# Strassen weight sums as additions, two of the four made by accumulating DMA transfers, in a decoder block on one core

## The chip, the cores and the metric

The kernel runs on one core of a Trainium2 chip. The metric is the device time of one execution in microseconds (us). TensorE (PE) does matrix products, VectorE (DVE) sums and differences of tiles, ScalarE (ACT) casts and activations, GpSimd (POOL) and SyncE (SP) mostly issue DMA transfers, each from a queue of its own that it works off in order.

## The reference

A hybrid decoder block on x of 512 positions by 2048 channels, in float32:

```python
proj = x @ w_in                       # 2048 x 7168
u_conv, u_pool, gates = proj[:, :2048], proj[:, 2048:3072], sigmoid(proj[:, 3072:])
y_conv = swish(layer_norm(causal_conv31(glu(u_conv)))) @ w_conv_out
y_pool = multiscale_pool(u_pool) @ w_pool * pool_scale
mix = (g_conv * y_conv + g_pool * y_pool) @ w_out
h = layer_norm(alpha * x + mix)
g, up = split(h @ w_ffn_in)           # 2048 x 11264
f = (silu(g) * up) @ w_ffn_out        # 5632 x 2048
out = layer_norm(alpha * h + f)
```

## The kernel before

Everything is laid out with channels on the 128 partitions. Each product is made in three passes over parts of type float32r: an operand is split into hi (a cast on ScalarE, line 85) and lo (the rest, a subtraction on VectorE, line 86), and a product is hi hi + hi lo + lo hi. Most stages run plain matmuls of 512 columns. Two stages, seven of the ten groups of gates (4 granules each) and the feed-forward's first product (22 groups of 4 granules), use Strassen's scheme in Winograd's form: the halves of positions, of input channels and of columns are 2 x 2 blocks, and seven products, numbered 1 to 7, of sums of input blocks by sums of weight blocks take the place of eight. A product of one granule is 12 matmuls of 256 columns, a granule 84. A group collects its seven products in seven PSUM banks over its four granules, and then drains them into sums (line 447 on VectorE). The products 1 and 2, which need unsummed weight blocks only, are done ahead in the first three feed-forward groups (EARLY = 3, `first_products`), so that these groups' granules have five products left, 60 matmuls. The input's sums are made once, by `sum_x` for the gates and `sum_s` for the feed-forward.

The weights come as a stream of blocks. `weights(n)` hands out block n; in a Strassen stage it prepares block n + 1 and loads block n + 2 before that. `load` (line 149) issues two transfers of 512 KB on SP's queue for a granule: (B11, B21) and (B12, B22). `combine` makes the four sums from them, all subtractions on VectorE (line 177), in a chain:

```python
sub(t1, b12, b11)
sub(t3, b22, b12)
sub(t2, b22, t1)
sub(t4, b21, t2)
```

Three of the four results take the place of a raw block; t2 goes to a small tile of its own (`unit`). Tiles come from the pool `pairs` (`d`, 46 buffers of 4 KB per partition), smaller ones from `units` (`u`, 10 of 2 KB). A framework places instructions on the engines and sets semaphores; what follows which on an engine is set when the program is built. GpSimd issues the stores of results that are read again later: gates, `conv`, `kept` (line 578) and `act` (line 664).

Of the kernel before, what the change touches and what calls it, by code (L numbers as in the profile page):

```python
# [18 lines left out]
P = 128  # L19
# [15 lines left out]
PLAIN = 3  # groups of gates whose product is plain  # L35
TAPS_AHEAD = 6

# columns of the packed per-channel parameters
# [12 lines left out]
def block_kernel(ctx, tc, xT, x, w1, wgs, wpool, wconv, wout, wfs, wfo, prm, rows, out):  # L51
    """Products run in three passes over float32r parts: a = hi + lo exactly, a b = hi hi + hi lo + lo hi.

    The feed-forward's first product goes through Strassen's scheme in Winograd's form, with the
    halves of positions, of input channels and of columns (gate, up) as its 2 x 2 blocks.
    """
    nc = tc.nc
    const = ctx.enter_context(tc.tile_pool(name="const", bufs=1))
    dp = ctx.enter_context(tc.tile_pool(name="pairs", bufs=46))
    up = ctx.enter_context(tc.tile_pool(name="units", bufs=10))  # L60
# [7 lines left out]
    def unit(dt=F32, shape=(512,)):  # L68
        return up.tile([P, *shape], dt, tag="u", name="u")

# [23 lines left out]
    def halves(ts):  # L94
        """Pairs as the list of their single tiles."""
        return [t[:, i, :] for t in ts for i in range(2)]

# [26 lines left out]
    for s in range(EARLY):  # L124
        use["fe", s] = len(blocks)
        blocks.extend(wfs[s, g, 0] for g in range(4))
# [16 lines left out]
    def load(n):  # L143
        if n < len(blocks) and n not in raw:
            src = blocks[n]
            if in_strassen(n):
                ts = [pair(shape=(2, 2, 256)) for _ in range(2)]
                for i in range(2):
                    nc.sync.dma_start(ts[i], src[i])
                raw[n] = ts  # L150
                return
            t = pair(shape=src.shape[1:])
            for k in (0, 1) if n == 0 else (slice(0, 2),):
                nc.sync.dma_start(t[:, k], src[:, k])
            raw[n] = t
# [14 lines left out]

    def combine(t, early):
        """The seven sums of weight blocks of Winograd's form, in parts, by the number of the product;
        without the first two where they are in use already."""
        b1, b2 = t
        b11, b21, b12, b22 = b1[:, 0], b1[:, 1], b2[:, 0], b2[:, 1]
        t1, t4, t3, t2 = b11, b21, b12, unit(shape=(2, 256))
        sub = lambda o, p, q: nc.vector.tensor_tensor(o, p, q, op=ALU.subtract)  # L177
        if not early:
            h1, l1 = split(b1)
        sub(t1, b12, b11)  # L180
        sub(t3, b22, b12)
        sub(t2, b22, t1)
        sub(t4, b21, t2)
        h2, l2 = unit(F32R, (2, 256)), unit(F32R, (2, 256))
        split_into(h2, l2, t2)
        h3, l3 = split(b2)
        h4, l4 = split(b1)
        ops = {6: (h2, l2), 7: (h3[:, 0], l3[:, 0]), 3: (h3[:, 1], l3[:, 1]),
               5: (h4[:, 0], l4[:, 0]), 4: (h4[:, 1], l4[:, 1])}
        if not early:  # L190
            ops.update({1: (h1[:, 0], l1[:, 0]), 2: (h1[:, 1], l1[:, 1])})
        return ops
# [21 lines left out]
    def spread(items, n):  # L214
        """The items in order over n steps."""
        return [items[i * len(items) // n:(i + 1) * len(items) // n] for i in range(n)]

    def channel_major(at, n_blocks, hi, lo, ps=None, half=None, during=()):
        """Weights stationary: four tiles of output channels by positions."""
        ps = ps or [bank() for _ in range(4)]  # L220
        sl = slice(0, 512) if half is None else slice(H * half, H * half + H)
        during = spread(during, n_blocks)
        for g in range(n_blocks):
            for f in during[g]:
                f()
            wh, wl = weights(at + g)
            for k in range(2):
                kt = 2 * g + k
                for c in range(4):
                    cs = slice(c * P, (c + 1) * P)  # L230
                    first = g == 0 and k == 0
                    last = g == n_blocks - 1 and k == 1
                    o = ps[c][:, sl]
                    nc.tensor.matmul(o, lhsT=wh[:, k, cs], rhs=hi[kt], start=first, stop=False)  # L234
                    nc.tensor.matmul(o, lhsT=wh[:, k, cs], rhs=lo[kt], start=False, stop=False)  # L235
                    nc.tensor.matmul(o, lhsT=wl[:, k, cs], rhs=hi[kt], start=False, stop=last)  # L236
        return ps

    def position_major(at, n_blocks, hi, lo, tbs, during=()):
        """Activations stationary: blocks of 128 positions by 512 output channels."""  # L240
# [17 lines left out]
    def mean_rstd(stats):  # L258
        """stats [P, n, 6] -> mean and 1/sqrt(var + eps).

        Three Newton steps y <- -y/2 (v y^2 - 3). The factor -1/2 of each is left out of y and put
        into v of the next (64 v, 16 v, 4 v) and into the start, which is -1/8 of the usual guess.
        """
# [44 lines left out]
    def conv_taps(u, c):  # L308
        """u, acc: one tile of channels by positions; the taps are queued."""
        u, acc = u  # L310

        def first():
            nc.scalar.activation(acc, u, AF.Identity, scale=col(C_DW + c * TAPS + TAPS - 1), bias=col(C_DWB + c))

        def tap(s):
            nc.vector.scalar_tensor_tensor(acc[:, s:], u[:, :S - s], col(C_DW + c * TAPS + TAPS - 1 - s),  # L316
                                           acc[:, s:], op0=ALU.mult, op1=ALU.add)

        background.append(first)
        for s in range(1, TAPS):  # L320
            background.append(lambda s=s: tap(s))
# [19 lines left out]
    # gates of the two branches, inputs of the pooling  # L341
# [10 lines left out]
    def pool_pair(i):  # L352
        """The steps for a pair of channel tiles."""
# [61 lines left out]
    def sum_x(i):  # L415
        """Winograd's sums of blocks of the input, for the channel tiles 2 i, 2 i + 1 of each half."""
# [3 lines left out]
        for o, a, b, op in ((a22, a21, a22, ALU.add), (a21, a11, a21, ALU.subtract),  # L420
                            (a11, a22, a11, ALU.subtract), (a12, a12, a11, ALU.subtract)):
            nc.vector.tensor_tensor(o, a, b, op=op)
# [9 lines left out]
    def products(ns, w, g, ps, operand):  # L432
        for n in ns:
            wh, wl = w[n]
            for j in range(2):
                h, l = operand(n, g, j)
                for p in range(2):
                    cs = slice(p * P, (p + 1) * P)
                    o = ps[n][:, p * H:(p + 1) * H]
                    # the start clears the marks of its whole bank, so one group spans both tiles  # L440
# [4 lines left out]

    def add(o, p, q):
        nc.vector.tensor_tensor(o, p, q, op=ALU.add)  # L447
# [17 lines left out]
    def strassen_gates(s, during=()):  # L465
# [10 lines left out]
        add(a, ps[6], a)  # L476
# [4 lines left out]
        add(b, ps[4], b)  # L481
# [59 lines left out]
    # by halves of the positions and tiles of 4 x 128 channels: whole, high part, low part  # L541
    af, ahi, alo = {}, {}, {}

    def norm1(t):
        """The steps of LayerNorm for a block of positions, into the layout by channels."""
# [6 lines left out]
        def chunk(c):  # L552
# [5 lines left out]
            parts = half == 0 or c > 1  # the fourth block goes into sums only  # L558
# [40 lines left out]
    def sum_s(i):  # L599
        """Winograd's sums of blocks of the input, for the channel tiles i and i + 2."""  # L600
        # each in the place of a block that is not needed whole any more
        a11, a12, a21, a22 = (0, i), (0, i + 2), (1, i), (1, i + 2)

        def step(n, o, a, b, op):
# [3 lines left out]
        return [lambda: step(1, a22, a21, a22, ALU.add), lambda: step(3, a21, a11, a21, ALU.subtract),  # L608
                lambda: step(2, a11, a22, a11, ALU.subtract), lambda: step(4, a12, a12, a11, ALU.subtract)]

    def operand(n, g, j):
        """The input's block or sum of the product n for a channel tile of the granule."""
# [8 lines left out]
    def gate1(ps, a, c11):  # L621
        """The sum of the first product, and the gate of the first half of the positions."""
# [6 lines left out]
    def first_products(s, during):  # L629
        ps = {n: bank() for n in (1, 2)}  # L630
        during = spread(during, 4)
        for g in range(4):
# [3 lines left out]
            products((1, 2), {1: (h[:, 0], l[:, 0]), 2: (h[:, 1], l[:, 1])}, g, ps, operand)  # L636
# [3 lines left out]
    def strassen_ffn(s, during=()):  # L640
# [13 lines left out]
        add(a, ps[6], a)  # L654
# [5 lines left out]
        add(b, ps[4], b)  # L660
# [36 lines left out]
    def restore(t, i):  # L697
        """Adds the scaled residual to the sums of a pair of column chunks."""
# [20 lines left out]
    def norm2(t):  # L719
        """The steps of the last LayerNorm for a block of positions."""  # L720
# [62 lines left out]
    # the last run goes block by block of positions  # L783
# [26 lines left out]
def _granules(w, cols):  # L810
    """[K, N] -> [len(cols), K/256, 128, 2, 512] with the given columns in each block."""
# [5 lines left out]
def _strassen_granules(w):  # L817
    """[K, 2, n, 256] -> [n, 4, 2 column halves, 128, 2 channel halves, 2, 256]."""
    w = w.reshape(2, 4, 2, P, *w.shape[1:])
    return w.transpose(5, 1, 4, 3, 0, 2, 6)  # L820
# [48 lines left out]
```

## Time and profile before

| | |
|---|---|
| median of 2 runs | 2304.68 us (2304.14 to 2305.23) |
| span of the profiled execution | 2303.7 us |
| TensorE busy | 2263.2 us, 98% |
| VectorE busy | 1657.7 us, 72% |
| ScalarE busy | 806.8 us, 35% |
| GpSimd busy | 132.0 us, 6% |
| read from HBM | 284.36 MB |

A row of busy time says how long an engine's instructions ran, not that anything waited for them. The chain that ended last says on what the end rests, and the waits of an engine say what it stood still for. Windows give the same numbers for one stretch of the execution, with the clock that TensorE was granted (PEclk: 1.00 is 2.4 GHz, 0.50 is 1.2 GHz) and the share of the 16 DMA engines in use.

### The profile page before, as it was taken

Reading aid. Unit: us, or ns where it says so; the run is one execution under the profiler, and the core shown is the slowest. Engines: PE = TensorE matmul, PEld = TensorE weight load, DVE = VectorE, ACT = ScalarE, POOL = GpSimd, SP = SyncE. Lnnn points to the kernel's source line nnn. Section 1 sums busy time; section 2 is a strip of 40 time slices with the busy share of each in tenths; the row PEclk is TensorE's granted clock in tenths of the full one; section 3 lists DMA queues with packets and bytes.
Section 4 is the critical chain, followed back from the end, with each engine's and each line's share of the span. In section 5 each row is a group of like instructions: output and inputs, shape, how many; then the busy total and the mean of one; then the engine's idle time right before and its main releaser. Section 6 shows DMA issues by size and latency. Waiting matters only on the chain.

```text
span 2303.7 us, 35226 instructions
## 1 busy us (share of the span) xinstructions
PE 2263.2 (98%) x14576; PEld 2072.1 (90%) x14576; DVE 1657.7 (72%) x2139; ACT 806.8 (35%) x952; POOL 132.0 (6%) x139
## 2 busy tenths in 40 slices
PE   8999999999999999799999999999999999999997
PEld 7888889999988888799999999999999888888885
DVE  4999788878677358989878787887878426363337
ACT  3212253444323236334434344343434333222211
POOL 0000000000000002400000000000000000000005
PEclk9999999999999999899999999999999999999998
DMA  6232253334746355243333333333334635454321
GB/s 259 90 102 76 101 204 128 134 119 158 272 157 218 110 181 203 92 158 121 117 128 112 109 129 119 112 118 128 112 109 142 211 105 201 134 172 135 108 83 73
DMA packets 90448, 319.15 MB, mean 139 GB/s; under 512 B 10544, under 2 KB 10672, under 8 KB 90288
## 3 DMA queue, kind: packets, MB, share of 16 engines
q1 hardware_dynamic: 77040, 273.71, 35.2%
q0 software_dynamic: 8352, 28.32, 3.2%
q10 hardware_dynamic: 4896, 14.88, 1.8%
q8 instruction: 114, 1.87, 0.3%
q14 instruction: 46, 0.38, 0.1%
HBM read 284.36 MB, written 32.51 MB: 138 GB/s over the span
## 4 chain that ended last, share of the span: by engine, by line
PE 93%; DVE 4%; issue 1%; ACT 1%; DMA 1%; POOL 0%; ACTq 0%; DVEq 0%
PE ps L444 16%; PE ps L442 16%; PE ps L443 16%; PE ps L775 6%; PE ps L776 6%; PE ps L774 6%; PE ps L236 5%; PE ps L235 5%; PE ps L234 5%; PE ps L253 3%; PE ps L254 3%; PE ps L255 3%; DVE d L86 1%; DVE d L177 1%; DMA d<-xT 1%
## 5 line engine op out<-in xcount | busy, mean ns | idle before, releaser
L86 DVE TENSOR_TENSOR d<-d 128x1024 fp32r<-128x1024 f32 (+1 forms) x607 | 736.7, 1231 | 397.1 <-ACT d L85 266.7
L85 ACT CAST d<-d 128x1024 fp32r<-128x1024 f32 (+1 forms) x615 | 630.1, 1047 | 885.5 <-DVE d L177 207.3
L444 PE MATMUL ps<-d 128*128 128x256 f32 x2784 | 788.4, 284 | 14.6 <-DVE d L86 14.3
L442 PE MATMUL ps<-d 128*128 128x256 f32 x2784 | 789.2, 284 | 1.4 <-ACT d L85 1.4
L443 PE MATMUL ps<-d 128*128 128x256 f32 x2784 | 788.7, 284 | 0.0
L444 PEld LDWEIGHTS ps<-d 128*128 128x128 f32 x2784 | 535.1, 193 | 16.7 <-DVE d L86 16.7
L442 PEld LDWEIGHTS ps<-d 128*128 128x128 f32 x2784 | 536.3, 193 | 1.9 <-ACT d L85 1.9
L443 PEld LDWEIGHTS ps<-d 128*128 128x128 f32 x2784 | 536.2, 193 | 0.1
L774 PE MATMUL ps<-d 128*128 128x512 f32 x640 | 249.0, 389 | 0.0
L775 PE MATMUL ps<-d 128*128 128x512 f32 x640 | 249.0, 389 | 0.0
L776 PE MATMUL ps<-d 128*128 128x512 f32 x640 | 248.1, 389 | 0.0
L234 PE MATMUL ps<-d 128*128 128x512 f32 x608 | 238.2, 392 | 5.1 <-ACT d L85 5.1
L235 PE MATMUL ps<-d 128*128 128x512 f32 x608 | 238.3, 392 | 1.6 <-DVE d L304 1.0
L236 PE MATMUL ps<-d 128*128 128x512 f32 x608 | 236.1, 392 | 0.4 <-DVE d L86 0.4
L447 DVE TENSOR_TENSOR u<-ps,u 128x512 f32<-128x512 f32 x188 | 127.1, 689 | 84.2 <-PE ps L444 81.8
L177 DVE TENSOR_TENSOR d<-d 128x512 f32<-128x512 f32 x232 | 167.6, 722 | 7.8 <-DMA d<-wfs 0.9
L316 DVE SCALAR_TENSOR_TENSOR d<-d,pr 128x510 f32<-128x510 f32 (+26 forms) x240 | 161.5, 765 | 0.6
L774 PEld LDWEIGHTS ps<-d 128*128 128x128 f32 x640 | 120.1, 188 | 25.0
L775 PEld LDWEIGHTS ps<-d 128*128 128x128 f32 x640 | 120.1, 188 | 24.9
L776 PEld LDWEIGHTS ps<-d 128*128 128x128 f32 x640 | 120.1, 188 | 24.9
L234 PEld LDWEIGHTS ps<-d 128*128 128x128 f32 x608 | 114.9, 189 | 28.4 <-ACT d L85 5.0
L235 PEld LDWEIGHTS ps<-d 128*128 128x128 f32 x608 | 114.8, 189 | 26.7 <-DVE d L86 1.5
(113 smaller groups left out, 2249.4 us busy)
## 6 DMA issues: line engine op xcount, KB each, us to landing
d<-wfs SPq DMA_DIRECT2D x188, 512.0 KB, 4.2
d<-wfo SPq DMA_DIRECT2D x88, 512.0 KB, 3.6
d<-wgs SPq DMA_DIRECT2D x56, 512.0 KB, 4.3
d<-w SPq DMA_DIRECT2D x55, 512.0 KB, 3.7
d<-wout SPq DMA_DIRECT2D x48, 512.0 KB, 3.9
d<-act SPq DMA_DIRECT2D x22, 512.0 KB, 4.6
act<-u POOLq DMA_DIRECT2D x41, 256.0 KB, 5.0
d<-gate SPq DMA_DIRECT2D x20, 512.0 KB, 4.7
```

The lines of the kernel that those rows point to most:

```text
L85: nc.scalar.copy(hi, src)
L86: (engine or nc.vector).tensor_tensor(lo, src, f32(hi), op=ALU.subtract)
L177: sub = lambda o, p, q: nc.vector.tensor_tensor(o, p, q, op=ALU.subtract)
L234: nc.tensor.matmul(o, lhsT=wh[:, k, cs], rhs=hi[kt], start=first, stop=False)
L235: nc.tensor.matmul(o, lhsT=wh[:, k, cs], rhs=lo[kt], start=False, stop=False)
L236: nc.tensor.matmul(o, lhsT=wl[:, k, cs], rhs=hi[kt], start=False, stop=last)
L442: nc.tensor.matmul(o, lhsT=wh[:, j, cs], rhs=h, start=first, stop=False)
L443: nc.tensor.matmul(o, lhsT=wh[:, j, cs], rhs=l, start=False, stop=False)
L444: nc.tensor.matmul(o, lhsT=wl[:, j, cs], rhs=h, start=False, stop=last)
L774: nc.tensor.matmul(ps[t], lhsT=hi[k][:, ts], rhs=wh[:, k, :], start=first, stop=False)
L775: nc.tensor.matmul(ps[t], lhsT=hi[k][:, ts], rhs=wl[:, k, :], start=False, stop=False)
L776: nc.tensor.matmul(ps[t], lhsT=lo[k][:, ts], rhs=wh[:, k, :], start=False, stop=last)
```

## The change

All four sums of weight blocks become additions. For that the sums of the input change their signs (`sum_x`, `sum_s`), and in the drain two additions become subtractions (products 6 and 4). The blocks of a granule lie in memory as B12, B22, B21, B11. A granule is loaded with three transfers: `t31` = (B22, B11) on SP's queue, 512 KB in pieces of 2 KB; then, on GpSimd's queue, an accumulating transfer that adds B12 to both halves of `t31`, so that it holds (B22 + B12, B11 + B12); and the triple `w3` = (B22, B21, B11) on SP's queue, 768 KB. VectorE makes the other two sums, `t24`, each from the one before it. Splits are then made of `t24`, of `t31` (1024 columns each) and of the triple (1536 columns, 512 in the early groups). The pools are recut: 40 pairs, 6 triples of 6 KB, 4 units.

```diff
-    dp = ctx.enter_context(tc.tile_pool(name="pairs", bufs=46))
-    up = ctx.enter_context(tc.tile_pool(name="units", bufs=10))
+    dp = ctx.enter_context(tc.tile_pool(name="pairs", bufs=40))
+    tp = ctx.enter_context(tc.tile_pool(name="triples", bufs=6))
+    up = ctx.enter_context(tc.tile_pool(name="units", bufs=4))
...
+    def triple(dt=F32):
+        return tp.tile([P, 3, 2, 256], dt, tag="w3", name="w3")
...
-        blocks.extend(wfs[s, g, 0] for g in range(4))
+        blocks.extend(wfs[s, g, :, 2:4] for g in range(4))
...
-                ts = [pair(shape=(2, 2, 256)) for _ in range(2)]
-                for i in range(2):
-                    nc.sync.dma_start(ts[i], src[i])
-                raw[n] = ts
+                w3, t31 = triple(), pair(shape=(2, 2, 256))
+                nc.sync.dma_start(t31, src[:, 1::2])
+                nc.gpsimd.dma_start(t31, src[:, 0:1].broadcast_to([P, 2, 2, 256]), accum_op=ALU.add)
+                nc.sync.dma_start(w3, src[:, 1:])
+                raw[n] = w3, t31
                 return
...
+        w3, t31 = t
+        w22, w21 = w3[:, 0], w3[:, 1]
+        t24 = pair(shape=(2, 2, 256))
+        add(t24[:, 0], t31[:, 1], w22)
+        add(t24[:, 1], t24[:, 0], w21)
+        h2, l2 = split(t24)
+        h1, l1 = split(t31)
+        h3, l3 = triple(F32R), triple(F32R)
+        n3 = 1 if early else 3
+        split_into(h3[:, :n3], l3[:, :n3], w3[:, :n3])
+        ops = {6: (h2[:, 0], l2[:, 0]), 4: (h2[:, 1], l2[:, 1]), 7: (h1[:, 0], l1[:, 0]), 5: (h1[:, 1], l1[:, 1])}
+        ops.update({n: (h3[:, i], l3[:, i]) for i, n in enumerate((3, 2, 1)[:n3])})
         return ops
...
-        for o, a, b, op in ((a22, a21, a22, ALU.add), (a21, a11, a21, ALU.subtract),
-                            (a11, a22, a11, ALU.subtract), (a12, a12, a11, ALU.subtract)):
+        for o, a, b, op in ((a22, a21, a22, ALU.subtract), (a21, a21, a11, ALU.subtract),
+                            (a11, a11, a22, ALU.subtract), (a12, a12, a11, ALU.subtract)):
...
-        add(a, ps[6], a)
+        sub(a, ps[6], a)
...
-        add(b, ps[4], b)
+        sub(b, ps[4], b)
...
-            products((1, 2), {1: (h[:, 0], l[:, 0]), 2: (h[:, 1], l[:, 1])}, g, ps, operand)
+            products((1, 2), {1: (h[:, 1], l[:, 1]), 2: (h[:, 0], l[:, 0])}, g, ps, operand)
```

What the change moves, at three places. First SP's queue in the middle of the feed-forward's first product. Before, the loads of granules follow each other, two to a granule (`d_12098` and `d_12099` are one granule):

```order
L149 DMA d_12098<-wfs 128x1024
L149 DMA d_12099<-wfs 128x1024
L149 DMA d_12232<-wfs 128x1024
L149 DMA d_12233<-wfs 128x1024
L149 DMA d_12341<-wfs 128x1024
```

Now each granule has a triple and a `t31` with neighbouring numbers: `w3_11720` and `d_11721` belong to granule 0 of a group, `w3_11824` and `d_11825` to granule 1, `w3_11953` and `d_11954` to granule 2, `w3_12057` and `d_12058` to granule 3, `w3_12161` and `d_12162` to granule 0 of the next group:

```order
L154 DMA w3_11824<-wfs 128x1536
L152 DMA d_11721<-wfs 128x2x512
L154 DMA w3_11953<-wfs 128x1536
L152 DMA d_11825<-wfs 128x2x512
L154 DMA w3_12057<-wfs 128x1536
L152 DMA d_11954<-wfs 128x2x512
L154 DMA w3_12161<-wfs 128x1536
L152 DMA d_12058<-wfs 128x2x512
L154 DMA w3_12265<-wfs 128x1536
L152 DMA d_12162<-wfs 128x2x512
```

The load of `t31` of a granule stands behind the triple's load of the granule after it. In the program the load of `w3_11953` waits for VectorE's second add of granule 0, and those of `w3_12057`, `w3_12161` and `w3_12265` for the last matmul of product 3 of granules 1, 2 and 3.

Second, GpSimd's queue at the same place. Before, it holds only the two stores of each group:

```order
L664 DMA act8_7829<-u_12189 256x1x256
L664 DMA act8_7829<-u_12186 256x1x256
L664 DMA act9_7830<-u_12650 256x1x256
L664 DMA act9_7830<-u_12647 256x1x256
L664 DMA act10_7831<-u_13111 256x1x256
```

Now the four accumulating transfers of a group (line 153) stand between the stores of one group and of the next:

```order
L666 DMA act8_7692<-u_11916 256x1x256
L666 DMA act8_7692<-u_11913 256x1x256
L153 DMA d_11825<-wfs 128x2x512
L153 DMA d_11954<-wfs 128x2x512
L153 DMA d_12058<-wfs 128x2x512
L153 DMA d_12162<-wfs 128x2x512
L666 DMA act9_7693<-u_12357 256x1x256
```

Third, TensorE in the same stage. Before, the products of one granule run in the order 1, 2, 6, 7, 3, 5, 4; here product 2 (bank `ps_12205`) passes into 6 (`ps_12206`) and 7 (`ps_12207`) of the same granule:

```order
L442 MATMUL ps_12205<-d_7570,d_12321 128x256
L443 MATMUL ps_12205<-d_7571,d_12321 128x256
L444 MATMUL ps_12205<-d_7570,d_12322 128x256
L442 MATMUL ps_12206<-d_8371,u_12329 128x256
L443 MATMUL ps_12206<-d_8372,u_12329 128x256
L442 MATMUL ps_12207<-d_8321,d_12333 128x256
```

Now products 1 (`ps_11931`) and 2 (`ps_11932`), with the split triple of granule 2 (`w3_12053`, `w3_12054`), stand ahead of product 6 (`ps_11933`) of granule 1 and between its first matmuls, and `d_11941` is the high part of `t24` of granule 1:

```order
L447 MATMUL ps_11931<-d_7350,w3_12053 128x256
L448 MATMUL ps_11931<-d_7351,w3_12053 128x256
L447 MATMUL ps_11933<-d_8114,d_11941 128x256
L448 MATMUL ps_11933<-d_8115,d_11941 128x256
L447 MATMUL ps_11937<-d_7820,d_11941 128x256
L448 MATMUL ps_11937<-d_7821,d_11941 128x256
L449 MATMUL ps_11931<-d_7350,w3_12054 128x256
L447 MATMUL ps_11932<-d_7433,w3_12053 128x256
```

So the products that need only the triple are moved ahead of those that need `t24`, into the granule before; `ps_11937` is product 4, which needs `t24` too.

## Rows read from the trace of the kernel before

**Rows 1.** The page: span, and part 1, busy time by engine.

```profile
span 2303.7 us, 35226 instructions
PE 2263.2 (98%) x14576; PEld 2072.1 (90%) x14576; DVE 1657.7 (72%) x2139; ACT 806.8 (35%) x952; POOL 132.0 (6%) x139
```

**Rows 2.** The page, part 4: the chain that ended last, shares of the span.

```profile
PE 93%; DVE 4%; issue 1%; ACT 1%; DMA 1%; POOL 0%; ACTq 0%; DVEq 0%
```

**Rows 3.** Windows, start:end and length in us, busy time (instructions) by engine.

```profile
core 0: us, PE busy (x) PEld busy (x) DVE busy (x) ACT busy (x) POOL busy (x), PEclk, DMA share, GB/s
...
1200.00:1400.00 200.00, 200.00 (x1669) 200.00 (x1669) 161.71 (x204) 79.21 (x95) 6.88 (x10) 1.00 0.34 119
...
945.40:952.10 6.70, 3.86 (x18) 3.86 (x19) 6.67 (x7) 4.18 (x5) 1.54 (x2) 0.50 0.05 11
...
1307.00:1308.00 1.00, 1.00 (x11) 1.00 (x10) 0.00 (x0) 0.00 (x0) 0.00 (x0) 1.00 0.89 352
```

**Rows 4.** Waits of TensorE over the whole span.

```profile
engine line waited for: us in total, times, longest us
PE ps L444 <- DVE d L86: 14.3, 5, 6.7
PE ps L234 <- ACT d L85: 5.1, 1, 5.1
PE ps L442 <- ACT d L85: 1.4, 2, 0.8
```

**Rows 5.** Groups by line and shape, 1200 to 1400 us (5 groups' worth, 20 granules).

```profile
L86 DVE TENSOR_TENSOR d<-d 128x1024 fp32r<-128x1024 f32 x60 | 72.3, 1219 | 14.1 <-ACT d L85 14.1
L85 ACT CAST d<-d 128x1024 fp32r<-128x1024 f32 x60 | 62.3, 1047 | 75.7 <-DVE d L177 33.0 <-DMA d<-wfs 16.9 <-PE ps L444 13.3
L177 DVE TENSOR_TENSOR d<-d 128x512 f32<-128x512 f32 x40 | 27.7, 692 | 1.2
...
L86 DVE TENSOR_TENSOR u<-u 128x512 fp32r<-128x512 f32 x20 | 13.7, 685 | 0.0
```

**Rows 6.** The chain that ended last, 926 to 953 us: start, length, what.

```profile
941.08 3.14 issue
944.23 2.82 DVE d L177
947.05 1.15 DVE d L86
948.19 0.04 issue
948.24 0.58 PE ps L444
```

**Rows 7.** Line 149 (loads of weights), 1344 to 1346 us: one granule's two loads.

```profile
L149 SPq DMA_DIRECT2D d<-wfs x2: 328/356/383, 1344.6 to 1345.0; - x2
...
DMA to landing us min/median/max: 3.5/3.9/4.3
```

**Rows 8.** Line 149, 1035 to 1036 us: a load by itself.

```profile
L149 SPq DMA_DIRECT2D d<-wfs x1: 327/327/327, 1035.0 to 1035.0; - x1
...
DMA to landing us min/median/max: 3.4/3.4/3.4
```

**Rows 9.** Tile `kept`, 908 to 909 us: a POOL store of 512 KB by itself.

```profile
L578 POOL DMA_DIRECT2D kept<-d x1: 577/577/577, 908.5 to 908.5; - x1
...
DMA to landing us min/median/max: 3.0/3.0/3.0
```

**Rows 10.** Tile `kept`, 852 to 857 us: four POOL stores of 512 KB.

```profile
L578 POOL DMA_DIRECT2D kept<-d x4: 531/635/741, 852.0 to 856.1; - x4
...
DMA to landing us min/median/max: 5.3/6.7/7.4
```

**Rows 11.** The page, part 6: DMA issues, KB each, us to landing.

```profile
act<-u POOLq DMA_DIRECT2D x41, 256.0 KB, 5.0
```

More of the change, by code (lines that the diff above doesn't have):

```diff
@@ L169, in prepare, with add, sub @@
         ready[n] = hi, lo
+    def add(o, p, q):
+        nc.vector.tensor_tensor(o, p, q, op=ALU.add)
+    def sub(o, p, q):
+        nc.vector.tensor_tensor(o, p, q, op=ALU.subtract)
     def combine(t, early):
[L174 to L191, printed above, removed]
+        w3, t31 = t
[10 more added lines that the diff above has]
+        ops.update({n: (h3[:, i], l3[:, i]) for i, n in enumerate((3, 2, 1)[:n3])})
         return ops
@@ L444, in products @@
                     nc.tensor.matmul(o, lhsT=wl[:, j, cs], rhs=h, start=False, stop=last)
-    def add(o, p, q):
-        nc.vector.tensor_tensor(o, p, q, op=ALU.add)
     during = [()] * PLAIN
@@ L606, in step @@
             sums[n, i] = split(af[o], nc.gpsimd)
-        return [lambda: step(1, a22, a21, a22, ALU.add), lambda: step(3, a21, a11, a21, ALU.subtract),
-                lambda: step(2, a11, a22, a11, ALU.subtract), lambda: step(4, a12, a12, a11, ALU.subtract)]
+        return [lambda: step(1, a22, a21, a22, ALU.subtract), lambda: step(3, a21, a21, a11, ALU.subtract),
+                lambda: step(2, a11, a11, a22, ALU.subtract), lambda: step(4, a12, a12, a11, ALU.subtract)]
     def operand(n, g, j):
@@ L653, in strassen_ffn @@
             gate1(ps, a, c11)
-        add(a, ps[6], a)
+        sub(a, ps[6], a)
         add(b, ps[7], a)
@@ L659, in strassen_ffn @@
         add(a, ps[5], b)
-        add(b, ps[4], b)
+        sub(b, ps[4], b)
         nc.scalar.activation(b, b, AF.Silu)
@@ L817, in _strassen_granules @@
 def _strassen_granules(w):
-    w = w.reshape(2, 4, 2, P, *w.shape[1:])
-    return w.transpose(5, 1, 4, 3, 0, 2, 6)
+    w = w.reshape(2, 4, 2, P, *w.shape[1:]).transpose(5, 1, 3, 0, 4, 2, 6)
+    return np.stack([w[:, :, :, k, c] for k, c in ((0, 1), (1, 1), (1, 0), (0, 0))], axis=3)
 def _by_tile(v):
```

## The prediction

> **What bounds the kernel now.** I read the page's first part and its chain [rows 1, 2]: TensorE is busy 98% of the span, and 93% of the chain that ended last is its matmuls. The windows [rows 3] say how: in 200 us of the feed-forward's first product TensorE stands still for nothing, at a granted clock of 1.00 (2.4 GHz), and does 1669 matmuls of 256 columns, 0.1198 us each. One Strassen product of a granule is 12 of them, T = 1.44 us; seven make a granule, 10.07 us, five an early one, 7.19 us. The waits of TensorE [rows 4] sum to some 22 us; the largest it had on weights in Strassen stages are two of 6.7 us. VectorE's rows [rows 5] give its load per granule: four subtractions of about 0.69, three parts of 1.22 and one of 0.69, 7.1 us under 10.07 us of matmuls. So VectorE isn't the bound, nor are the transfers; work that is taken from VectorE there buys nothing as long as TensorE never waited for it. Everything that TensorE waited for is about 1% of the time: no edit that leaves the matmuls as they are can bring 2%, which is about what a measurement of this kernel can tell from no change.
>
> **What the change removes.** The matmuls are the same in number and shape. VectorE loses two of four sums per granule, and its parts come to 2 x 1.22 for the two pairs and, for the triple of 1536 columns, 1.5 x 1.22 = 1.83: 1.4 + 2.4 + 1.8 = 5.6 us per full granule. That is hidden either way. What can be had is the wait at the start of the first early group: in the chain there [rows 6] the sums and the parts of weights stand in a row (2.82 and 1.15 us behind 3.14 us of issue), TensorE waits 6.7 us, and behind it the clock is at 0.50 (1.2 GHz) for 6.7 us, of which some 3 us of matmuls run at half pace, 1 to 2 us lost [rows 3]. With half the sums, and these on loaded blocks, this wait can go, and with it the two short ones (1.4 us together [rows 4]): 11 us, or nothing if what VectorE does for the input's sums is late in its place. I take 11 off. The other 6.7 us wait hangs on the first block of normed input and stays. The other signs of sums in the input and the drains swap one operation for another of the same size: nothing. The early stage uses the same two blocks in other positions: nothing. Seven fewer buffers than before for pairs and units are in part given to triples; in the plain stages weight loads are still released dozens of matmuls ahead, so I put that at nothing, and it costs at most the start of each such stage.
>
> **What it adds: a chain of transfers.** Before, a granule's raw weights come with two loads issued 0.4 us apart on SP's queue; the second lands 4.3 us after its own issue, 4.7 after the first's [rows 7]. Now three transfers fetch 1.75 MB instead of 1 MB, and two depend on each other: t31 (512 KB) must land before POOL's accumulating transfer of another 512 KB may start, and this must land before VectorE's first add. And the rows of SP show that each t31 load stands behind the triple's load of the next granule, which waits: in the four granules of a group for the second add of the granule before, or for the last matmul of a product 3. So t31 of a granule is not asked for two granules ahead but at that trigger.
>
> Let W be the time from the trigger until the accumulating transfer has landed. Its terms: 0.1 us of issue; t31 behind the triple's 768 KB instead of behind 512 KB, so 4.7 plus 256 KB at 352 GB/s (the rate with the queue full [rows 3], 0.75 us) = 5.5 us; then the accumulation, which no row shows. Its low end is a plain POOL transfer of 512 KB in a quiet place, 3.0 us [rows 8]. Its high end is the slowest of four POOL transfers of that size beside others, 7.4 us [rows 9]; 256 KB stores take 5.0 us in the middle [rows 10]. Below 3.0 there is no reason to go: the transfer has a fixed part that the plain one has too. In between I take a single quiet load of 512 KB, 3.4 us [rows 11], plus 1.5 us for another 512 KB at 352 GB/s, since the old sum must be read as well as the new block: 4.9 us. W is then 8.6, 10.5 or 13.0 us.
>
> The Trainium skill has for this, in "Collectives: The Full Stack", section "The bandwidth ceiling: the fold count and why AG ≠ RS ≠ AR", that the addition of a reducing transfer costs no cycles, but that it needs two source reads and so runs at about half the rate of a copy. No run here shows an accumulating transfer; if the rule holds, it speaks for the middle value.
>
> **What of W is covered.** When the accumulation has landed, two adds (1.4 us [rows 5]) and ScalarE's cast (1.05 us) come before product 6 may start: W + 2.45. From the order of TensorE I count the work between trigger and product 6, for granules 0 to 3 of a full group:
> - Granule 1: the trigger is the second add of granule 0, 1.05 us ahead of its product 6; then come five products, product 3 of this granule, product 1 of the next, less a matmul: 9.95 us. Stall: W + 2.45 - 1.05 - 9.95 = W - 8.5.
> - Granule 2: the trigger is the end of product 3 of granule 1; eight products and two matmuls follow (11.7 us) and the stall just named. Its own is below zero: none.
> - Granule 3: from product 3 of granule 2 on, eight products and seven matmuls, 12.3 us, and no stall within. Stall: W - 9.8.
> - Granule 0 of the next group: eight products, 11.5 us, and the stall of granule 3 within. Stall: W - 9.0 less that stall, so 0.8 us once W is over 9.8.
>
> The sum is 2 W - 17.5 us per full group (nothing below W = 8.5): 0.1, 3.5 or 8.5 us. There are 7 groups of gates and 19 of the feed-forward, 26: 3, 91 or 221 us. An early group has five products per granule, 2.9 us less cover, in two waits like that of granule 1: 2 (W - 8.5 + 2.9) = 2 W - 11.2, which is 6.0, 9.8 or 14.8 us, for three groups 18, 29 or 44 us.
>
> The drain, POOL's other transfers and the tail: POOL now issues 116 more transfers of about 0.6 us each [rows 8], on an engine that is 6% busy. Its stores of activations stand ahead of an accumulation in its queue, but wait for a drain that is done in time. I put this at nothing; if it isn't, it is part of the high end.
>
> Sum: 2303.7 - 11 + 91 + 29 = 2413 us for the profiled execution; it lies 1.0 us under the median of the runs, so 2414 us.
>
> **The rivals.**
> *The accumulation is as fast as a plain transfer* (ends within 2%). Then W is about 8.6 and the sum is 2303.7 - 11 + 3 + 18 + 1 = 2315 us. For it: the quiet POOL row of 3.0 us. Against it: the same kind of transfer takes 5 us and more in most places, and here the triple's load is still on its way. The point from which it decides is W = 9.4, where 26 x 1.3 + 3 x 7.6 - 11 is 46 us, 2%: an accumulation of 3.8 us. The Trainium skill's "DMA: Bandwidth & Descriptors", section "Anatomy of one DMA — SWDGE (gpsimd) path", gives about 2.0 us and the bytes at 436 GB/s for a transfer on this path, an estimate of 3.2 us here; the quiet row agrees with its 3.0, and by that rule the time would be about 2320.
>
> *The accumulation is slower than two passes*, 7.4 us or more, because the two loads of the next granule and it share the same 16 engines. W is 13 or over: 2560 us and up. For it: the slowest store; against it: the queues are idle two thirds of this stage (a DMA share of 0.34 [rows 3]).
>
> *The clock falls in the new stalls.* After the two idles of 6.7 us it was at half; after those of 0.8 us and less it was not. Stalls of 2.0 and 1.5 us per group lie between. If one of them per full group brings a half-speed stretch of 6.7 us, it loses 3.4 us each time: 26 x 3.4 = 88 us more, 2502.
>
> *Faster by over 2%* would need a matmul that is quicker than 0.1198 us; nothing in the change makes one. Between 0 and 1% of gain stays possible if W is under 8.5: 2293 at best.
>
> **How the numbers follow.** The forecast's case (W between 9.4 and 13) has 0.6, its own range is 2350 to 2560; the fast accumulation 0.23; the very slow one 0.1; the falling clock 0.06; a gain over 2%, 0.01. Slower is 0.6 + 0.1 + 0.06 = 0.76, within 2% 0.23. The predicted time is 2414. The range reaches from 2312, which takes in nearly all of the fast case, to 2560; left out are the slow case and the little below.
>
> **What would show it.** Right: in the same 200 us stretch some 1535 matmuls instead of 1669 (10.07 against 10.07 + 3.5 / 4 per granule); waits of TensorE for ScalarE's casts of about 120 us in all, most of them on the first matmul of product 6, two or three per group of 1 to 2 us; ScalarE or VectorE waiting for the accumulating transfer; VectorE less busy by some 150 us and no better for it; an issue row of that transfer with some 4.9 us to landing. Wrong: a landing of 3.8 us or less with TensorE at 98% still; or the t31 load asked for long before its trigger, so that W is hidden whatever it is; or stalls that stand at SP's queue, with the triple's load as their cause, and not at the accumulation.

## The result, and the profile after

The changed kernel takes 2706.89 us (2705.79 to 2707.99) against 2304.68: a ratio of 1.174, 95% interval 1.171 to 1.178. It is slower, as forecast, but by 402 us instead of 109, outside the range. (One correction to the prediction's references: its groups 8 to 11 are named one off. Where it says [rows 8] the row stands in group 9, for 9 in 10, for 10 in 11, and for 11 in 8.)

The page of the changed kernel, part 1, the shares of its chain, and three lines of part 6 (DMA issues, KB each, median us to landing):

```profile
span 2706.2 us, 34670 instructions
...
PE 2419.2 (89%) x14576; PEld 2197.5 (81%) x14576; DVE 1510.5 (56%) x1803; ACT 799.7 (30%) x848; POOL 275.6 (10%) x255
...
PE 54%; DMA 27%; DVE 10%; issue 4%; ACT 4%; SPq 1%; POOLq 0%; POOL 0%; DVEq 0%; ACTq 0%
...
w<-wfs SPq DMA_DIRECT2D x88, 768.0 KB, 4.7
d<-wfs SPq DMA_DIRECT2D x100, 512.0 KB, 5.5
d<-wfs POOLq DMA_DIRECT2D x88, 512.0 KB, 6.2
```

Against [rows 1] TensorE has the same 14576 matmuls and is busy 156 us longer; VectorE lost 147 us of work, and nothing came of it. The chain went 93% through TensorE [rows 2]; now a quarter of it is transfers.

The waits of TensorE, the two largest groups (us in total, times, longest), and two windows of the feed-forward's first product:

```profile
PE ps L447 <- ACT d L89: 242.5, 119, 4.7
PE ps L449 <- DVE d L90: 13.4, 5, 6.5
```

```profile
1200.00:1400.00 200.00, 168.93 (x1216) 164.94 (x1216) 98.25 (x104) 58.26 (x56) 22.67 (x22) 0.88 0.55 146
1400.00:1600.00 200.00, 167.50 (x1260) 163.69 (x1259) 106.38 (x112) 58.07 (x56) 25.24 (x24) 0.93 0.58 151
```

All waits of TensorE sum to 269.5 us, against 23.5 before. So the 402.5 us between the spans are 246 us of waits, 156 us by which TensorE is busy longer with the same work, and half a microsecond of other things. In 200 us it does 1216 and 1260 matmuls, not 1669 [rows 3]; 1260 matmuls at 0.1198 us are 151 us, and it was busy 167.5, at a granted clock of 0.93 over the window.

The mean clock of the changed kernel, then of the kernel before, and the matmuls around one stall:

```profile
core 0: 2706.2 us, clock 0.939
core 0: 2303.7 us, clock 0.994
...
1457.95 0.28 PE L447 MATMUL ps<-d,w 128*128 128x256 f32 x1
1460.78 0.39 PE L447 MATMUL ps<-d 128*128 128x256 f32 x1 [2.55 <-ACT d L89]
1461.00 0.28 PE L448 MATMUL ps<-d 128*128 128x256 f32 x1
```

The 156 us have two parts. A mean clock of 0.939 means 329 us at 1.2 GHz (27 before). In these the trace has TensorE busy for 280 us with 1281 matmuls, which at 0.1198 us would be 153: 127 us lost, against 4 before, so the slow clock costs about 122 us. The other part is starting again. The last matmul before a stall counts to its (modelled) end, 0.28 us, where in the stream the next one starts after 0.12; and the first behind the stall holds the next back for 0.22. That is 0.26 us for each stall: for 133 waits against 14 before an estimate of 31 us.

One stall, in the chain that ended last from 1445 to 1461 us (start, length, what):

```profile
1445.52 0.34 SPq L154
1445.86 0.05 issue
1445.96 5.36 DMA d<-wfs
1451.39 0.50 issue
1451.88 6.27 DMA d<-wfs
1458.18 0.70 DVE d L177
1458.90 0.70 DVE d L177
1459.68 1.05 ACT d L89
1460.78 0.39 PE ps L447
```

This is the chain that the prediction wrote down, link by link (a few pieces of less than 0.1 us are left out): the triple's load is let go, then t31's load 0.44 us behind it (5.36 us), 0.56 us until GpSimd issues, the accumulation (6.27 us), two adds, the cast, product 6. From the trigger to the landing, W is 12.6 us.

Windows on either side of three stalls of that group:

```profile
core 0: us, PE busy (x) PEld busy (x) DVE busy (x) ACT busy (x) POOL busy (x), PEclk, DMA share, GB/s
1454.00:1456.00 2.00, 2.00 (x19) 2.00 (x18) 0.69 (x1) 0.63 (x1) 0.00 (x0) 1.00 1.08 183
1449.00:1450.00 1.00, 0.99 (x9) 0.79 (x8) 0.88 (x1) 0.01 (x1) 0.00 (x0) 1.00 0.98 375
1458.20:1460.80 2.60, 0.05 (x2) 0.02 (x1) 1.40 (x3) 1.12 (x2) 0.00 (x0) 1.00 0.97 374
1461.90:1465.50 3.60, 3.60 (x20) 3.60 (x20) 2.09 (x4) 1.16 (x1) 1.20 (x1) 0.53 0.16 25
1471.80:1473.50 1.70, 0.33 (x2) 0.30 (x2) 1.23 (x3) 1.68 (x3) 0.42 (x1) 1.00 0.89 207
1474.00:1484.00 10.00, 9.88 (x81) 9.82 (x81) 3.27 (x3) 1.54 (x2) 1.25 (x1) 1.00 0.70 192
1484.20:1488.40 4.20, 0.04 (x1) 0.04 (x1) 1.45 (x3) 1.14 (x2) 0.00 (x0) 1.00 0.87 303
1489.30:1492.60 3.30, 3.30 (x19) 3.30 (x18) 3.12 (x3) 1.33 (x1) 1.22 (x1) 0.52 0.01 4
```

About 1 us behind the end of an idle of 2.6 us, and of one of 4.2 us, TensorE runs at about half the clock (1.2 GHz); behind the one in the window of 1.7 us it stays at 2.4 GHz. The first two lines show the accumulation by itself (its share of the queues is full and it moves 183 GB/s) and plain loads (375 GB/s).

### The profile page after: what moved, and what is told of

It reads as the page before. It is cut to its first block, busy times and chain, and to the rows that moved or that the text cites. A ratio compares the mean times of both kernels' runs of the same rounds, so it can differ in the third digit from the quotient of the medians.

```text
span 2706.2 us, 34670 instructions
## 1 busy us (share of the span) xinstructions
PE 2419.2 (89%) x14576; PEld 2197.5 (81%) x14576; DVE 1510.5 (56%) x1803; ACT 799.7 (30%) x848; POOL 275.6 (10%) x255
## 4 chain that ended last, share of the span: by engine, by line
PE 54%; DMA 27%; DVE 10%; issue 4%; ACT 4%; SPq 1%; POOLq 0%; POOL 0%; DVEq 0%; ACTq 0%
DMA d<-wfs 20%; DMA d<-wgs 6%; PE ps L447 6%; PE ps L778 5%; PE ps L777 5%; PE ps L776 5%; PE ps L448 5%; PE ps L449 5%; PE ps L240 5%; PE ps L241 5%; PE ps L239 5%; DVE d L177 4%; ACT d L89 2%; PE ps L259 2%; PE ps L260 2%
## 5 line engine op out<-in xcount | busy, mean ns | idle before, releaser
L90 DVE TENSOR_TENSOR d<-d 128x1024 fp32r<-128x1024 f32 (+1 forms) x503 | 609.7, 1238 | 450.6 <-ACT d L89 320.2
L447 PE MATMUL ps<-d 128*128 128x256 f32 x1952 | 616.6, 317 | 242.9 <-ACT d L89 242.5
L89 ACT CAST d<-d 128x1024 fp32r<-128x1024 f32 (+1 forms) x511 | 516.8, 1046 | 1035.3 <-DVE d L177 541.1
L447 PEld LDWEIGHTS ps<-d 128*128 128x128 f32 x1952 | 426.5, 219 | 268.7 <-ACT d L89 268.4
L448 PE MATMUL ps<-d 128*128 128x256 f32 x1952 | 596.4, 307 | 0.0
L449 PE MATMUL ps<-d 128*128 128x256 f32 x1952 | 574.4, 308 | 13.7 <-DVE d L90 13.4
L448 PEld LDWEIGHTS ps<-d 128*128 128x128 f32 x1952 | 425.7, 218 | 0.0
L449 PEld LDWEIGHTS ps<-d 128*128 128x128 f32 x1952 | 409.1, 216 | 19.2 <-DVE d L90 18.8
L449 PE MATMUL ps<-d,w 128*128 128x256 f32 x1296 | 375.4, 290 | 0.0
L447 PE MATMUL ps<-d,w 128*128 128x256 f32 x1296 | 374.4, 289 | 0.0
L448 PE MATMUL ps<-d,w 128*128 128x256 f32 x1296 | 372.9, 288 | 0.0
L177 DVE TENSOR_TENSOR d<-d,w 128x512 f32<-128x512 f32 x232 | 160.2, 690 | 320.3 <-DMA d<-wfs 240.6
L90 DVE TENSOR_TENSOR w<-w,w 128x1536 fp32r<-128x1536 f32 (+1 forms) x116 | 190.9, 1646 | 208.2 <-ACT w L89 106.3
L449 PEld LDWEIGHTS ps<-d,w 128*128 128x128 f32 x1296 | 257.9, 199 | 0.3 <-DVE w L90 0.2
L447 PEld LDWEIGHTS ps<-d,w 128*128 128x128 f32 x1296 | 256.9, 198 | 0.1
L448 PEld LDWEIGHTS ps<-d,w 128*128 128x128 f32 x1296 | 255.5, 197 | 0.1
L239 PE MATMUL ps<-d 128*128 128x512 f32 x608 | 238.4, 392 | 10.5 <-ACT d L89 9.9
```

The lines of the kernel that those rows point to most:

```text
L89: nc.scalar.copy(hi, src)
L90: (engine or nc.vector).tensor_tensor(lo, src, f32(hi), op=ALU.subtract)
L447: nc.tensor.matmul(o, lhsT=wh[:, j, cs], rhs=h, start=first, stop=False)
L448: nc.tensor.matmul(o, lhsT=wh[:, j, cs], rhs=l, start=False, stop=False)
L449: nc.tensor.matmul(o, lhsT=wl[:, j, cs], rhs=h, start=False, stop=last)
```

## The experiments

The theory: the accumulating transfer hangs on t31's load, and the pair is asked for too late, because of where t31 stands in SP's queue; the stalls follow from W, and each longer one costs again by a slow clock. The rivals: the 0.75 MB more per granule (and the slow accumulation) fill the queues whatever the order is; the signs; the recut pools.

**The signs alone.** The kernel before with additions in place of the four subtractions, and the other signs in the input's sums and the drain (cut to the weights' sums):

```diff
-        sub = lambda o, p, q: nc.vector.tensor_tensor(o, p, q, op=ALU.subtract)
+        sub = lambda o, p, q: nc.vector.tensor_tensor(o, p, q, op=ALU.add)
```

Expected:

> The kernel before with the signs alone changed: four additions of weights instead of subtractions, the other signs in the input's sums and in the drain; loads, blocks and pools as before. Every theory that puts the loss on transfers expects no change: 2304 us within 0.5%. If signs or the changed places of the input's sums cost anything, it shows here.

Measured: 2304.57 us, ratio 1.000 (0.999 to 1.001). The signs cost nothing.

**All additions on VectorE.** The changed kernel without the accumulating transfer, so with its pools, its blocks and its triple, and 1 MB per granule:

```diff
-                nc.sync.dma_start(t31, src[:, 1::2])
-                nc.gpsimd.dma_start(t31, src[:, 0:1].broadcast_to([P, 2, 2, 256]), accum_op=ALU.add)
+                nc.sync.dma_start(t31[:, 0], src[:, 0])
...
+        add(t31[:, 1], t31[:, 0], w3[:, 2])
+        add(t31[:, 0], t31[:, 0], w22)
         add(t24[:, 0], t31[:, 1], w22)
```

Expected:

> The changed kernel without the accumulating transfer: B12 is loaded alone (256 KB) into the place of the first half of t31, the triple as before, and VectorE makes all four sums as additions; 1.0 MB per granule as in the kernel before, the changed kernel's pools and signs. Theory: no chain of two dependent transfers is left; W falls from 12.6 to about 5.5 us, no stall is left in the Strassen stages: 2285 to 2320 us. Rival (pools cut to 40 and 4, or the triples' late release, are what stalls): over 2400 us.

Measured: 2325.16 us, ratio 1.009 (1.007 to 1.011). In the middle of the feed-forward's first product it is at the full rate again:

```profile
1400.00:1600.00 200.00, 200.00 (x1669) 200.00 (x1668) 159.37 (x184) 76.76 (x75) 6.91 (x10) 1.00 0.36 119
```

So 382 of the 402 us go with the accumulating transfer and the bytes that come with it. The 20 us that stay (the time is 5 us over the expected range) belong to what this kernel keeps of the change (pools, blocks, three buffers per triple). Of TensorE's waits they are 13 us more than before, 3 at the very first weights and most of the rest in the early groups; which part of the change makes them was not tried.

**A plain transfer in the accumulation's place**, to price the addition (two of the sums are left out):

```diff
-                nc.gpsimd.dma_start(t31, src[:, 0:1].broadcast_to([P, 2, 2, 256]), accum_op=ALU.add)
+                nc.gpsimd.dma_start(t31, src[:, 0:1].broadcast_to([P, 2, 2, 256]))
```

Expected:

> The changed kernel with the accumulating transfer replaced by a plain one of the same shape on the same queue, which overwrites t31 with B12 (two of the sums are left out). It prices the addition. Theory (the addition halves the rate, since the old values are read too): the transfer lands in 3.5 to 4.5 us instead of 6.2, W is about 10.3, the stalls are 2 W - 17.5 = 3 us per full group instead of 8.7, and as they are about 2 us each the clock falls behind few of them: 2390 to 2480 us. Rival (GpSimd's path or the 2 KB pieces set the 6.2 us): it lands in about 6 us and the time stays near 2700.

Measured: 2578.93 us in one run. Line 153 from 1300 to 1700 us:

```profile
L153 POOL DMA_DIRECT2D d<-wfs x32: 722/722/737, 1310.3 to 1682.6; - x32
...
DMA to landing us min/median/max: 4.4/4.6/6.3
```

The addition costs 1.6 us of landing (6.2 to 4.6) and 0.5 us of GpSimd's issue (1.22 to 0.72). Not all of that need be the addition: in the trace the plain transfer goes in 128 packets of 4 KB, the accumulation in 256 of 2 KB. But even the plain transfer takes 4.6 us here, not 3.0 as the quiet store [rows 9], so W is still 11 us and the time 274 us over the kernel before: TensorE waits 199 us in all and is busy 97 us longer than before. The measured time is 99 us over the expected range. The waits grew by 175 us, where the prediction's formulas give 109 for the expected W of 10.3 and 149 for one of 11; and 175 us ran at 1.2 GHz (a mean clock of 0.966), so the clock falls behind these stalls too.

**An accumulating transfer of half the size.** Only the first half of t31 gets B12 by the transfer; VectorE makes three sums:

```diff
-                nc.gpsimd.dma_start(t31, src[:, 0:1].broadcast_to([P, 2, 2, 256]), accum_op=ALU.add)
+                nc.gpsimd.dma_start(t31[:, 0], src[:, 0], accum_op=ALU.add)
...
-        add(t24[:, 0], t31[:, 1], w22)
+        add(t24[:, 0], t31[:, 0], t31[:, 1])
+        sub(t31[:, 1], t24[:, 0], w22)
         add(t24[:, 1], t24[:, 0], w21)
```

Expected:

> The changed kernel with an accumulating transfer of half the size: B12 is added to the first half of t31 only (256 KB), VectorE makes the other three sums. SP's queue is as in the changed kernel. If the 6.2 us of the accumulation are about 2.4 us fixed and 512 KB at half a copy's rate, this one lands in about 4.3 us, W is 10.7 us instead of 12.6, and with the sum W + 2.45 + 0.7 for the third addition the time is 2540 to 2620 us, like that with the plain transfer. If the price is one per transfer and not per byte, it lands in about 6 us and the time is 2700 us or more.

Measured: 2569.07 us in one run, inside the expected range, and line 153 from 1300 to 1700 us:

```profile
L153 POOL DMA_DIRECT2D d<-wfs x33: 850/880/934, 1312.9 to 1695.0; - x33
...
DMA to landing us min/median/max: 4.1/4.2/4.3
```

256 KB less are 2.0 us less (6.2 to 4.2), which is 131 GB/s for the accumulation's bytes; the rest, 2.2 us, is the part that doesn't go with the size. The Trainium skill ("Collectives: The Full Stack", section "The bandwidth ceiling: the fold count and why AG ≠ RS ≠ AR") says of the reducing transfers of a ring between cores that they run at about half a copy's rate, as the addition needs two source reads. By the windows above (183 against 375 GB/s) the rate is about half here too; by the two sizes it is 131 against the 352 GB/s of [rows 3], 0.37. That the second read is the reason no run here shows.

**t31 ahead of its triple.** The first test of the queue's order: everything as in the changed kernel, but on SP's queue the triple's load of a granule stands behind the t31 load of the same granule (`keep_in_program_order` pins an instruction behind what was written before it for the same engine):

```diff
-                nc.sync.dma_start(w3, src[:, 1:])
+                tc.keep_in_program_order(nc.sync.dma_start(w3, src[:, 1:]))
```

Expected:

> The changed kernel with one difference: on SP's queue the triple's load of a granule is pinned behind the t31 load of the same granule, so t31 no longer stands behind the next granule's triple; bytes, accumulating transfers, sums and pools are the same. Theory (a chain of transfers asked for too late, W = 12.6 us from the trigger, and the clock that falls behind its stalls): t31 is asked for when the parts of the sums of two granules before are made, about 18.9 us ahead of its product 6, against W + 2.45 = 15 us; TensorE's waits fall from 270 us to under 40, the granted clock is 1.00 in the stage, the time is 2290 to 2330 us. Rival 1 (the 0.75 MB more per granule and the slow accumulation load the queues): the waits stay, 2600 us or more. Rival 2 (pools, signs): stays at about 2707 too.

Measured: 2539.19 us, ratio 1.102 (1.101 to 1.104): 168 us gained with the same transfers, which speaks against the rivals of the bytes and of the pools, but far from 2330. The theory missed what came next. TensorE's largest wait, and the chain from 1430 us on:

```profile
PE ps L449 <- DVE w L90: 114.4, 49, 3.9
...
1430.80 0.73 POOL act L666
1431.53 3.32 issue
1434.85 0.02 POOLq L153
1434.87 0.09 POOL act L666
1434.96 0.51 issue
...
1435.48 8.25 DMA d<-wfs
...
1444.45 1.68 DVE w L90
```

The accumulation for the next group had its t31 at 1426.7 us and stood until 1435.5 behind GpSimd's two stores of the group that was ending (line 666), which wait for the drain. It was a new wait on a queue which the prediction had put at nothing; VectorE makes the triple's low part (`w`, line 90) behind the add that waits for it, so TensorE's wait bears that name.

**GpSimd's queue in the order of the program too**, so that accumulations asked for early stand ahead of these stores (the stores of gates and of activations are pinned like the transfer; against the changed kernel, cut):

```diff
-                nc.gpsimd.dma_start(t31, src[:, 0:1].broadcast_to([P, 2, 2, 256]), accum_op=ALU.add)
-                nc.sync.dma_start(w3, src[:, 1:])
+                tc.keep_in_program_order(
+                    nc.gpsimd.dma_start(t31, src[:, 0:1].broadcast_to([P, 2, 2, 256]), accum_op=ALU.add))
+                tc.keep_in_program_order(nc.sync.dma_start(w3, src[:, 1:]))
...
```

Expected:

> As the run with t31 ahead of its triple, and in addition GpSimd's queue keeps the order of the program: the accumulating transfers stand ahead of the stores of the group that ends while they are wanted (in that run an accumulation stood 9 us behind two stores that waited for the drain). Bytes, accumulations and sums are those of the changed kernel. Theory (what costs is only where the two transfers stand in their queues, and the clock that falls behind the stalls): stalls in the Strassen stages fall from 150 us to under 40, the granted clock is at 0.98 or more, 2300 to 2350 us. Rival (three quarters of a megabyte more per granule, half of it at the accumulation's slow rate, can't be moved in 10 us beside the rest): waits stay over 100 us, 2450 us or more.

Measured: 2508.73 us, ratio 1.089 (1.087 to 1.091); 30 us gained, and another miss: by its time and by its waits (151 us in all) the run lies where the rival was expected. So GpSimd's queue was a small part of what the run before had left. TensorE's largest wait is for the triple's low part as before, and VectorE's rows at the end of a group give another reason for it than the transfers (start, length, line, idle before):

```profile
PE ps L450 <- DVE w L90: 89.0, 34, 5.5
PE ps L448 <- ACT d L89: 32.0, 11, 6.2
```

```profile
1420.42 1.29 DVE L178 TENSOR_TENSOR u<-ps,u 128x512 f32<-128x512 f32 x2 [0.63 <-PE ps L450]
1421.62 0.68 DVE L662 TENSOR_TENSOR u<-u 128x512 f32<-128x512 f32 x1
1422.22 0.68 DVE L181 TENSOR_TENSOR u<-ps,u 128x512 f32<-128x512 f32 x1
1422.82 0.68 DVE L178 TENSOR_TENSOR d<-d,w 128x512 f32<-128x512 f32 x1
1423.42 1.75 DVE L90 TENSOR_TENSOR w<-w,w 128x1536 fp32r<-128x1536 f32 x1
```

The low part of the next granule's triple (L90, `w`) could be made from 1417.7 us on, when its cast had ended, 5.7 us earlier, but stands behind the drain (`u<-ps,u`), which waits for the last product.

**The drain pinned behind the next granule's parts**, in both Strassen stages, on top of the last run:

```diff
-        add(c11, ps[2], a)
+        tc.keep_in_program_order(nc.vector.tensor_tensor(c11, ps[2], a, op=ALU.add))
```

Expected:

> As the run with GpSimd's queue in program order, and the first addition of each group's drain is pinned behind what was traced on VectorE before it, so that the next granule's two additions and the low part of its triple no longer stand behind the seven operations of the drain. In that run TensorE waited 89 us in 34 waits for the low part of a triple, which VectorE made behind the drain although its cast was done 6 us earlier. Theory (what is left is VectorE's row order at the ends of groups, and the clock behind it): about 3.4 us of waiting and 2 us of slow clock per group go, 2370 to 2430 us. Rival (the transfers are the limit): within 1% of 2509 us, with the wait named after another engine.

Measured: 2416.09 us, ratio 1.049 (1.047 to 1.051), as expected. From 1200 to 1800 us, in the middle of the stage, nothing is left of the loss (the last line is of the accumulations from 1300 to 1700 us):

```profile
1200.00:1400.00 200.00, 200.00 (x1668) 199.93 (x1667) 132.86 (x144) 75.55 (x75) 30.36 (x29) 1.00 0.72 197
1400.00:1600.00 200.00, 200.00 (x1669) 200.00 (x1668) 133.44 (x145) 74.97 (x74) 30.95 (x29) 1.00 0.72 195
1600.00:1800.00 200.00, 200.00 (x1669) 200.00 (x1669) 132.73 (x143) 76.28 (x75) 31.68 (x30) 1.00 0.72 196
...
DMA to landing us min/median/max: 5.9/6.2/8.1
```

The same 1.75 MB per granule, the same accumulations of 6.2 us, and TensorE at the rate and the clock of [rows 3]. Neither the bytes nor the accumulation's own speed bound this stage: only when they are asked for, and what VectorE does first. The waits that remain, 72 us more than before, are in the gates, the early groups and just behind these; they weren't pursued, and there the rival is not ruled out.

**The plain transfer again, with GpSimd's queue in order** (two of the sums are left out, and the drain isn't pinned; the rest of the edit is that of the run with GpSimd's queue in order):

```diff
-                nc.gpsimd.dma_start(t31, src[:, 0:1].broadcast_to([P, 2, 2, 256]), accum_op=ALU.add)
...
+                tc.keep_in_program_order(
+                    nc.gpsimd.dma_start(t31, src[:, 0:1].broadcast_to([P, 2, 2, 256])))
...
```

Expected:

> The run with GpSimd's queue in program order, with the accumulating transfer replaced by a plain one of the same shape (t31 is overwritten with B12, so two of the sums are left out). In the changed kernel this replacement brought 129 us. If the accumulation is covered once it is asked for in time, it brings under 30 us here: 2480 to 2510 us. If the accumulation's time or its load on the queues is what is left, it brings 80 us or more: 2430 us or less.

Measured: 2474.46 us in one run, 34 us less than with the addition. That lies between the two expectations, nearer to the one that says that the accumulation is mostly covered; in the changed kernel the same edit brought 128 us.

## Why the prediction was wrong

- *What bounds the kernel, and VectorE's relief.* Right: 147 us of VectorE's work went, and gave nothing.
- *The chain, its trigger, and the stalls as a function of W.* Right. With the measured W of 12.6 us the prediction's own formulas give 26 x (2 x 12.6 - 17.5) + 3 x (2 x 12.6 - 11.2) = 242 us of stalls; measured are 246 more than before. The stalls also sit where they were forecast: from 1400 to 1600 us in granules 1, 3 and 0, none in granule 2. In the run with half an accumulation (W = 10.6, and 0.7 us for its third sum) the formulas give 167 us and the waits grew by 165; with the plain transfer they fall short, 149 against 175. That t31's place in SP's queue makes the trigger is shown by the run that changed nothing else (168 us).
- *"In between I take ... 4.9 us".* This term was mis-sized. The accumulation takes 6.2 us, t31 with its issue 5.8 instead of 5.6, and 0.56 us between the two were left out: W is 12.6, not 10.5. It cost 242 - 120 = 122 us of the error. The 1.5 us for the second read was taken at a load's full rate; the accumulation moves its bytes at 131 to 183 GB/s, and a plain transfer in its place needs 4.6 us with no addition in it.
- *"The clock falls in the new stalls", with 0.06 and as a case apart.* This is the step that failed. It isn't a rival of the stalls but their companion, and the sum had no term for it: at W = 12.6 most stalls are 1.4 to 4.2 us, and the slow clock cost 122 us. Starting again behind the stalls had no term either, and took some 31 us. The rival's own price, one slow stretch per full group, was 88 us; and the range's upper end (2560) had W = 13 without any of it. The changed kernel's trace ties the two together: from 300 to 2150 us (waits less than 1 us apart taken as one stall) none of the 13 stalls under 1.5 us had a fall of the clock in it or in the 3.5 us behind it, 64 of the 71 stalls of 2 us and more had one, and each of the 66 falls stands at a stall of 1.5 us or more. Stalls of three origins (the transfers, GpSimd's stores, VectorE's drain) came with a lower clock, and where the same transfers made no stall it was 1.00. An experiment that keeps the stalls and lets TensorE work through them was not made, so that the idle itself is the cause rests on this.
- *"I take 11 off".* Wrong: the wait of 6.5 us in the first early groups is still there (L449 behind L90), and the first weights' wait grew (5.1 to 8.0 us).
- *"I put this at nothing"* of GpSimd's queue. In the changed kernel that held by the chain shown; but it is what came late next as soon as t31 was asked for earlier.
- *"Seven fewer buffers".* The pairs and units are twelve fewer (46 and 10, now 40 and 4). What the change keeps beside the transfer, the pools among it, was put at nothing; the run with all additions on VectorE is 20 us slower than the kernel before.

Of the 293 us between the forecast and the measured span 122 are the accumulation, 122 the clock, 31 the starts and 11 what was taken off. The sum with 242 us of stalls, and with the 156 us measured for the clock and the starts put in: 2303.7 + 242 + 156 = 2702 us, against a span of 2706.2.

## What to carry to other kernels

A transfer that must wait for another one lengthens the time that a tile has to be asked for ahead (here from 4.7 to 12.6 us); before a sum is moved to such a pair, find the instruction that lets the first one go, and what stands before it in its queue. A stall on a busy TensorE is to be priced by more than its idle time: here 246 us of waits brought 122 us of slow clock and some 31 us of starting again. And when one order is put right, read the next: here SP's queue (168 us), GpSimd's queue (30) and VectorE's drain (93) each hid the next.

## What was not expected of the hardware

An accumulating transfer of 512 KB from HBM into SBUF takes 6.2 us at the median (5.9 to 7.2), a plain one on the same queue 4.6, an accumulating one of 256 KB 4.2; issuing it occupies GpSimd for 1.22 us against 0.72. The Trainium skill's rule for this path ("DMA: Bandwidth & Descriptors", section "Anatomy of one DMA — SWDGE (gpsimd) path": 2.0 us and the bytes at 436 GB/s) would give an estimate of 3.2 us for 512 KB and of 2.6 for 256 KB, and fits none of these three; the 2.2 us that the two accumulations leave for a fixed part are near its 2.0.
